# Retention steps over seven side steps instead of four, and mixer outputs in DRAM by halves

## The chip, the cores and the metric

The kernel runs on one core of one Trainium2 chip, in one launch. The metric is device time in microseconds. TensorE is called PE, VectorE DVE, ScalarE ACT, GpSimd POOL, SyncE SP, as in the profile.

## The reference

A hybrid decoder layer on 2048 tokens of width 1024, with 16 learned meta tokens in front, all float32:

```python
h = layer_norm(concat([meta, x]), ln_in)
u, q, k, v, g = split(h @ w_in)            # 256, then 4 x 768 (6 heads of 128)
y_s5  = s5_mixer(u)                        # 16 groups of 16 channels, 64 complex states, scan over tokens
y_ret = retention_mixer(q, k, v, g)        # per head, chunks of 128 tokens, below
h = layer_norm(alpha * h + concat([y_s5, y_ret]) @ w_out, ln1)
h = layer_norm(alpha * h + square(relu(h @ w_up)) @ w_down, ln2)   # d_ff = 4096
return h[:, 16:]

# retention, for a chunk, after rotating q and k:
scores = (q @ k.T) * dmat                  # decayed causal mask
out    = scores @ v + (q @ state) * xi
state  = gamma ** 128 * state + (k * zeta).T @ v
y      = silu(g) * group_norm(out)
```

## The kernel before

**Blocks and phases.** The tokens are worked in two blocks of 1024 (8 tiles of 128 tokens). For each block phase 1 makes the mixers' outputs, phase 2 the output projection with the residual and ln1, phase 3 the MLP. In phase 1 the six heads follow one another: for each tile of a head 24 matmuls make q, k and v (each float32 product is three matmuls of split operands, `mm3`), then `ret_start` begins the retention of that tile; after the fourth and the eighth tile `gates` makes the gate of 512 tokens with 24 more matmuls (in block 1's first head both gates come first).

**The order by hand.** All engines work in program order, which the kernel writes itself. `tick()` is called at set places between matmuls: for a tile once after its first 12 matmuls and once behind `ret_start`; for a gate after 12 matmuls and at its end; in `phase2_open` after the marked products. A tick raises `now`, runs the functions that `defer(k, fn)` has put down for that time or before, the one with the lowest time first, moves the background work (`bg`: the S5 mixer) by one step (`pump`), and feeds weights: a DMA into `wraw`, a cast on ACT and a subtraction on DVE or POOL (L205, L207). In block 0 a gate of the heads after the first has one more pump.

**Retention of a tile.** `ret_start` (L641) scales v on ACT and rotates q and k on DVE (L651 to L654), then defers stage b by 2: two transposes into a bank `pt` of the `sm` pool and a copy on ACT (L666). Stage c, 1 later: scores and k-v product into one bank `pS` (L671, L672), the masked scores `sT` on DVE (L674). Stage d, 1 later: the output into `pO` (L680, L681), the update of the state R from `pS` (L682), statistics and a copy into `o4` (L685 to L687). With the fourth tile of a half `group_norm` follows: a power on POOL, the scaling 2 later, and 4 later the transposes (L718), the affine map on ACT (L720), the product with the gate on DVE (L722) and, one tick on, the store of `y` to DRAM (L723). `meta_head` starts R from the 16 meta tokens, its matmul (L636) 2 ticks behind (1 in the first head).

**Buffers.** PSUM has two pools of four banks, `big` and `sm`. Four retention tiles, norm transposes and S5's matmuls share `sm`; the `big` banks take projections. `o4` has one buffer, `qk` two, `v2` three, `sT` and `qkT` two.

**S5.** `s5_prepare` builds the matrices of the 16 groups in block 0, with one sm bank `pk` a group; `s5_run` then runs them, up to three side by side, each with a bank `pa` (L1035) in its third step and `py` (L1067) in its sixth; a new group starts every 2 steps in block 0, every 4 in block 1. At the end it stores the S5 output (L1134) from `y5o`, one buffer.

**Into phase 2.** `phase2_ahead` loads the mixer outputs of tiles 0 and 1 for the heads that are done; `phase2_split` splits them; `phase2_open` drains S5, runs the products of the first seven channel groups (KORDER) for four groups of sums, flushes all deferred functions, and only then loads and splits the last one (head 5). `phase2` loads ln1's weights, tile 2 (eight DMAs, L1202), the residual tiles (L1207), finishes the open groups (L1211), and splits tile 2 (L1140) behind the first two.

Of the kernel before, what the change touches and what calls it, by code (L numbers as in the profile page):

```python
# [19 lines left out]
NM = 16  # L20
# [30 lines left out]
class Builder:  # L51
# [315 lines left out]
    def build(self):  # L367
        nc, a = self.nc, self.a
        with self.tc.manual_schedule():
# [13 lines left out]
            self.h_d = [dt(f"h{t}", [128, D]) for t in range(NB * NT)]  # L383
            self.y_d = [[dt(f"y{b}_{k}", [128, TB]) for k in range(8)] for b in range(NB)]
            self.s_d = [[dt(f"sum{b}_{x}", [128, 4, 2, 512]) for x in range(5)] for b in range(NB)]
# [230 lines left out]
    def meta_head(self, h, part):  # L616
        nc, p1 = self.nc, self.p1
        ps = self.big()
        mh, ml = self.mT
        self.mm3(ps[:NM, :256], [(mh[:, k, :], ml[:, k, :], part(k, 0, 128, 384), part(k, 1, 128, 384))  # L620
                                 for k in range(8)])
        c, s = self.ropem[:, 0:64], self.ropem[:, 64:128]
        t1 = p1.tile([NM, 2, 64], F32, tag="t1", name="mt1")
        t2 = p1.tile([NM, 2, 64], F32, tag="t2", name="mt2")
        km = p1.tile([NM, 2, 64], F32, tag="qk", name="mk", bufs=2)
        vm = p1.tile([NM, 128], F32, tag="v2", name="mv", bufs=3)
        kin = ps[:NM, 0:128].rearrange("p (a d) -> p a d", a=2)
        nc.scalar.activation(out=vm, in_=ps[:NM, 128:256], func=AF.Copy, scale=self.cols[:NM, 24 + h:25 + h])
        nc.vector.tensor_tensor(out=t1, in0=kin, in1=c.unsqueeze(1).to_broadcast([NM, 2, 64]), op=ALU.mult)
        nc.vector.tensor_tensor(out=t2, in0=kin, in1=s.unsqueeze(1).to_broadcast([NM, 2, 64]), op=ALU.mult)  # L630
        nc.vector.tensor_tensor(out=km[:, 0, :], in0=t1[:, 0, :], in1=t2[:, 1, :], op=ALU.subtract)
        nc.vector.tensor_tensor(out=km[:, 1, :], in0=t1[:, 1, :], in1=t2[:, 0, :], op=ALU.add)

        def fin():
            pr = self.sm()
            nc.tensor.matmul(pr[:, :128], km.rearrange("p a d -> p (a d)"), vm, start=True, stop=True)  # L636
            nc.scalar.copy(self.R[h], pr[:, :128])
        self.defer(1 if h == 0 else 2, fin)


    def ret_start(self, b, h, t, ps):  # L641
        nc, p1 = self.nc, self.p1
        v2 = p1.tile([128, 128], F32, tag="v2", name="v2", bufs=3)
        nc.scalar.activation(out=v2, in_=ps[:, 256:384], func=AF.Copy, scale=self.cols[:, h:h + 1])
# [3 lines left out]
        t2 = p1.tile([128, 4, 64], F32, tag="t2", name="t2")  # L648
        qk = p1.tile([128, 4, 64], F32, tag="qk", name="qk", bufs=2)
        src = ps[:, 0:256].rearrange("p (a d) -> p a d", a=4)  # L650
# [4 lines left out]
        q = qk.rearrange("p a d -> p (a d)")  # L655
        if t % 4 == 0:
            self.o4 = p1.tile([128, 4, 128], F32, tag="o4", name="o4")
            self.mv4 = self.small([128, 4, 2], "gn_mv", 3)
        o4, mv4 = self.o4, self.mv4

        def stage_b():
            pt = self.sm()
            nc.tensor.transpose(pt[:, 0:128], q[:, 0:128], self.ident)
            nc.tensor.transpose(pt[:, 128:256], q[:, 128:256], self.ident)
            qkT = p1.tile([128, 256], F32, tag="qkT", name="qkT", bufs=2)
            nc.scalar.copy(qkT, pt[:, 0:256])  # L666
            self.defer(1, lambda: stage_c(qkT))

        def stage_c(qkT):
            pS = self.sm()  # L670
            nc.tensor.matmul(pS[:, 0:128], qkT[:, 128:256], qkT[:, 0:128], start=True, stop=True)  # L671
            nc.tensor.matmul(pS[:, 128:256], q[:, 128:256], v2, start=True, stop=True)  # L672
            sT = p1.tile([128, 128], F32, tag="sT", name="sT", bufs=2)
            nc.vector.scalar_tensor_tensor(out=sT, in0=pS[:, 0:128], scalar=float(GAMMA[h] ** -128),  # L674
                                           in1=self.mask, op0=ALU.mult, op1=ALU.mult)
            self.defer(1, lambda: stage_d(qkT, pS, sT))

        def stage_d(qkT, pS, sT):
            pO = self.sm()
            nc.tensor.matmul(pO[:, 0:128], sT, v2, start=True, stop=False)  # L680
# [9 lines left out]

        self.defer(2, stage_b)

# [8 lines left out]
    def group_norm(self, b, h, nb, o4, mv4):  # L701
# [6 lines left out]
        def scale():  # L708
            nc.vector.tensor_scalar(out=sc, in0=sc, scalar1=self.cols[:, 6 + h:7 + h], scalar2=None, op0=ALU.mult)
            for i in range(4):  # L710
                nc.vector.tensor_scalar(out=o4[:, i, :], in0=o4[:, i, :], scalar1=mv4[:, i, 0:1],
                                        scalar2=sc[:, i:i + 1], op0=ALU.subtract, op1=ALU.mult)
        self.defer(2, scale)

        def fin():
# [6 lines left out]
            nc.vector.tensor_tensor(out=y, in0=y, in1=self.sgate.pop((b, h, nb)), op=ALU.mult)  # L722
            self.defer(1, lambda: nc.sync.dma_start(out=self.y_d[b][2 + h][:, nb * 512:(nb + 1) * 512], in_=y))  # L723
        self.defer(4, fin)

# [159 lines left out]
    def s5_prepare(self):  # L885
# [33 lines left out]
        def group(g):  # L919
# [9 lines left out]
            def double(k):  # L929
# [18 lines left out]
            yield  # L948
            pk = self.sm()
            flat = lambda z: z.rearrange("p m c -> p (m c)")  # L950
# [4 lines left out]
            yield  # L955
            V.tensor_tensor(out=kz[:, 0:GC], in0=pk[:GC, 0:GC], in1=dd[:, g, :], op=ALU.add)
            S.copy(kz[:, GC:128], pk[:GC, GC:128])
# [13 lines left out]
        nc.sync.dma_start(out=dT, in_=a["s5_dT"])  # L971
        dd = p1.tile([GC, NG, GC], F32, name="dd")
        V.tensor_tensor(out=dd, in0=self.ident[:GC, :GC].unsqueeze(1).to_broadcast([GC, NG, GC]),
                        in1=dT.unsqueeze(2).to_broadcast([GC, NG, GC]), op=ALU.mult)
        self.swap = p1.tile([128, 128], F32, name="swap")
# [46 lines left out]
    def s5_group(self, b, g, y):  # L1022
# [6 lines left out]
        if b == 0:  # L1029
            uT = p1.tile([128, 130], F32, tag="uTm", name="uTm", bufs=3)  # L1030
            S.copy(uT[:, :128], self.uT[:, g])
            S.copy(uT[:, 128:130], self.umT[:, g])
# [39 lines left out]
    def s5_run(self, b):  # L1072
# [46 lines left out]
        for oc in range(2):  # L1119
            on = p1.tile([128, TB], F32, tag="misc", name="y5o")  # L1120
            onv = on.rearrange("p (c j) -> p j c", j=8)
            for n in range(2):
# [10 lines left out]
                yield  # L1133
            nc.sync.dma_start(out=self.y_d[b][oc], in_=on)  # L1134

# [9 lines left out]
    def y_load(self, b, ks):  # L1145
        for k in ks:
            self.nc.sync.dma_start(out=self.yraw[:, :, k, :],
                                   in_=self.y_d[b][k][:, 0:256].rearrange("p (t c) -> p t c", t=2))

# [16 lines left out]
    def phase2_open(self, b):  # L1166
# [5 lines left out]
        k0 = self.cover  # L1172
        self.y_load(b, KORDER[k0:7])
        for t, hf in groups:
            ps = self.open[t, hf] = self.big()
            self.mm3(ps, self.out_pairs(t, hf, 0, k0), marks=(1, 3, 6), last=False)
        if k0 < 7:
            for t in range(2):
                self.y_split(raw[:, t, 0:2], 0, 2, self.ys[t])
            for t, hf in groups:  # L1180
                self.mm3(self.open[t, hf], self.out_pairs(t, hf, k0, 7), marks=(1,), first=False, last=False)
        self.flush()
        self.y_load(b, KORDER[7:])
        for t in range(2):
            self.y_split(raw[:, t, 7:8], 7, 8, self.ys[t])

    def out_pairs(self, t, hf, k0, k1):
# [4 lines left out]
    def phase2(self, b):  # L1192
# [6 lines left out]
        def load(t):  # L1199
            raw = self.stp.tile([128, 8, 128], F32, tag="tmp", name="yraw", bufs=2)  # L1200
            for k in range(8):
                nc.sync.dma_start(out=raw[:, k, :], in_=self.y_d[b][k][:, t * 128:(t + 1) * 128])  # L1202
            return raw
# [360 lines left out]
```

## Time and profile before

| | |
|---|---|
| median of 3 runs | 2450.3 us (2446.16 to 2452.24) |
| profiled execution | 2449.24 us, its span 2447.5 us |
| granted clock, mean of the span | 0.987 |
| phase 1 of block 0, of block 1 | 0 to 510 us, 1280 to 1690 us |
| DVE, POOL busy | 66%, 11% |
| DMA | 313.13 MB, 128 GB/s over the span |

The profile page gives each engine's busy time as a share of the span, and the span in 40 slices; the trace answers who waited for whom, what ran in a stretch, and in what order. In rows of an order of time the number in brackets is how long that engine stood idle before the operation, with the operation that released it. "PEld" is PE's weight load, "SPq" a DMA issue on SP. A granted clock of 1.00 is 2.4 GHz, the other level is 1.2 GHz.

### The profile page before, as it was taken

The page shows a single profiled execution, that of the slowest core. Times are in us where ns is not written, and L with a number is a line of the kernel's source. Part 1 is how long each engine was busy: PE and PEld are TensorE (multiplying, and loading weights), DVE is VectorE, ACT ScalarE, POOL GpSimd, SP SyncE. Part 2 cuts the span into 40 slices and gives each one's busy share as a digit, 9 for nine tenths or more (in the row PEclk, how much of TensorE's full clock was granted, in tenths as well). Part 3 has the DMA queues.
Part 4 walks back from the last instruction along what each step waited for, and adds up shares of the span by engine and source line. Part 5 has one row for each costly group of instructions (what it writes and reads, how often), then busy time and mean ns, then how long its engine had stood idle before and what let it go on. Part 6 is the DMA issues. An engine that isn't in the chain of part 4 may idle for free. (4 is left out here: it accounts for less than half of the span.)

```text
span 2447.5 us, 31696 instructions
## 1 busy us (share of the span) xinstructions
PE 2344.7 (96%) x11596; PEld 2007.5 (82%) x11596; DVE 1615.6 (66%) x3491; ACT 668.4 (27%) x1431; POOL 263.4 (11%) x334
## 2 busy tenths in 40 slices
PE   6889999899999999999999999999999999999998
PEld 5778889778878888888888999987887888888886
DVE  6867757666867776766585455565686666566657
ACT  3323323222321232123232222222232122212222
POOL 2322222301000000000030011100100000000004
PEclk8999999999999999999999999999999999999999
DMA  5132253352464546453442322234246343434332
GB/s 202 66 103 83 87 116 114 91 169 73 138 241 146 167 161 202 141 165 112 146 164 92 89 75 79 78 101 153 74 139 239 114 155 112 137 113 155 112 129 86
DMA packets 166972, 313.13 MB, mean 128 GB/s; under 512 B 18544, under 2 KB 59280, under 8 KB 166560
## 3 DMA queue, kind: packets, MB, share of 16 engines
q1 hardware_dynamic: 166816, 311.11, 39.4%
q8 instruction: 91, 1.49, 0.3%
q14 instruction: 65, 0.53, 0.1%
HBM read 256.25 MB, written 55.84 MB: 128 GB/s over the span
## 5 line engine op out<-in xcount | busy, mean ns | idle before, releaser
L357 PE MATMUL big<-pg,act 128*128 128x384 f32 x2304 | 457.0, 348 | 0.8 <-ACT act L340 0.6
L357 PE MATMUL big<-act,pg 128*128 128x512 f32 x1632 | 425.1, 395 | 2.4 <-DVE act L341 2.4
L357 PE MATMUL big<-pg,q 128*128 128x512 f32 x1728 | 412.2, 390 | 0.0
L357 PEld LDWEIGHTS big<-pg,act 128*128 128x128 f32 x2304 | 403.4, 192 | 4.7 <-DVE act L341 1.5
L357 PEld LDWEIGHTS big<-pg,q 128*128 128x128 f32 x1728 | 323.8, 188 | 67.1
L357 PEld LDWEIGHTS big<-act,pg 128*128 128x128 f32 x1632 | 303.9, 189 | 66.9 <-DVE act L341 2.9
L357 PE MATMUL sm<-pg,q 128*128 128x512 f32 x1344 | 322.8, 389 | 0.0
L357 PEld LDWEIGHTS sm<-pg,q 128*128 128x128 f32 x1344 | 252.3, 188 | 52.4
L281 POOL TENSOR_TENSOR ln_rs<-ln_rs,mhalf 128x1 f32<-128x1 f32 (+1 forms) x49 | 51.3, 1047 | 1481.5 <-DVE ln_rs L280 1481.4
L357 PE MATMUL sm<-act,pg 128*128 128x512 f32 x672 | 188.7, 389 | 0.0
L357 PE MATMUL big<-pg,yt 128*128 128x512 f32 x768 | 183.2, 397 | 1.6 <-DVE yt L1140 1.5
L207 DVE TENSOR_TENSOR pg<-wraw,pg 128x512 fp32r<-128x512 f32 x238 | 151.6, 688 | 39.7 <-ACT pg L205 39.7
L357 PEld LDWEIGHTS big<-pg,yt 128*128 128x128 f32 x768 | 145.1, 191 | 33.6 <-DVE yt L1140 3.3
L205 ACT CAST pg<-wraw 128x512 fp32r<-128x512 f32 x272 | 153.2, 619 | 68.1 <-DMA wraw<-in_w_down_dram 27.2
L219 ACT CAST pg<-q 128x512 fp32r<-128x512 f32 x112 | 69.4, 622 | 355.8 <-DVE q L216 355.8
L1288 ACT CAST q<-q 128x512 fp32r<-128x512 f32 x128 | 79.5, 621 | 272.3 <-DVE q L1286 257.4
L357 PE MATMUL sm<-q,pg 128*128 128x512 f32 x504 | 144.6, 395 | 7.5 <-DMA q<-sum 4.0
L1456 DVE TENSOR_TENSOR acc<-acc,big 128x512 f32<-128x512 f32 x128 | 87.0, 684 | 94.7 <-PE big L357 94.6
L1290 DVE TENSOR_TENSOR q<-q 128x512 fp32r<-128x512 f32 x128 | 88.7, 693 | 91.9 <-ACT q L1288 89.0
L357 PEld LDWEIGHTS sm<-act,pg 128*128 128x128 f32 x672 | 126.1, 188 | 26.1
L357 PE MATMUL big<-q,pg 128*128 128x512 f32 x504 | 143.8, 394 | 0.0
L220 DVE TENSOR_TENSOR pg<-q,pg 128x512 fp32r<-128x512 f32 x112 | 76.3, 692 | 82.2 <-ACT pg L219 77.8
(235 smaller groups left out, 2915.2 us busy)
## 6 DMA issues: line engine op xcount, KB each, us to landing
q<-sum SPq DMA_DIRECT2D x336, 256.0 KB, 5.3
wraw<-in_wup_dram SPq DMA_DIRECT2D x64, 512.0 KB, 4.0
wraw<-in_w_down_dram SPq DMA_DIRECT2D x64, 512.0 KB, 4.2
wraw<-in_wslab_dram SPq DMA_DIRECT2D x48, 512.0 KB, 3.6
sum<-q SPq DMA_DIRECT2D x64, 256.0 KB, 2.3
smat<-mat SPq DMA_DIRECT2D x32, 256.0 KB, 3.8
wraw<-in_w_out_dram SPq DMA_DIRECT2D x16, 512.0 KB, 3.7
acc<-h SPq DMA_DIRECT2D x16, 512.0 KB, 3.8
```

What stands on the lines that cost most here:

```text
L205: nc.scalar.copy(pg[z][:, 0, :], raw[0][:, z * 512:z * 512 + 512])
L207: e.tensor_tensor(out=pg[z][:, 1, :], in0=raw[0][:, z * 512:z * 512 + 512], in1=pg[z].bitcast(F32)[:, 0, :], op=ALU.subtract)
L219: nc.scalar.copy(pg[:, 0, :], x)
L220: self.post.append(lambda: nc.vector.tensor_tensor(out=pg[:, 1, :], in0=x, in1=pg.bitcast(F32)[:, 0, :], op=ALU.subtract))
L281: nc.gpsimd.tensor_tensor(out=rs[:n, 0:1], in0=rs[:n, 0:1], in1=self.mhalf[:n, 0:1], op=ALU.pow)
L357: nc.tensor.matmul(ps, l, r, start=(i == 0), stop=(i == n - 1), skip_group_check=more)
L1288: nc.scalar.copy(hi, x)
L1290: nc.vector.tensor_tensor(out=lo, in0=x, in1=hi.bitcast(F32), op=ALU.subtract)
L1456: nc.vector.tensor_tensor(out=acc, in0=acc, in1=ps, op=ALU.add)
```

## The change

Stages b, c and d of a tile come 3, 5 and 7 ticks behind `ret_start` (before 2, 3 and 4), with four buffers for `qk` and five for `v2`; `o4` is taken in stage d. The meta matmul comes 4 ticks behind (1 in the first head). Group norm's transposes come at 3.9 (before 4), which at a tick sorts them ahead of a stage d; in the first head of block 1 the scaling comes after 1 tick and the transposes at 1.9. `pk` takes a `big` bank. The table `dd` goes: its product is made in the operation that adds it. `uTm` has two buffers. The mixer outputs lie in DRAM as tiles of 512 tokens, the S5 output is stored in two parts, and the last head's channel group of tiles 0 and 1 is loaded with the others, and split before the flush.

```diff
-            self.y_d = [[dt(f"y{b}_{k}", [128, TB]) for k in range(8)] for b in range(NB)]
+            self.y_d = [[[dt(f"y{b}_{k}_{n}", [128, 512]) for n in range(2)] for k in range(8)] for b in range(NB)]
...
-        self.defer(1 if h == 0 else 2, fin)
+        self.defer(1 if h == 0 else 4, fin)
...
-        v2 = p1.tile([128, 128], F32, tag="v2", name="v2", bufs=3)
+        v2 = p1.tile([128, 128], F32, tag="v2", name="v2", bufs=5)
...
-        qk = p1.tile([128, 4, 64], F32, tag="qk", name="qk", bufs=2)
+        qk = p1.tile([128, 4, 64], F32, tag="qk", name="qk", bufs=4)
...
-            self.defer(1, lambda: stage_c(qkT))
+            self.defer(2, lambda: stage_c(qkT))
...
-            self.defer(1, lambda: stage_d(qkT, pS, sT))
+            self.defer(1.9, lambda: stage_d(qkT, pS, sT))
 
         def stage_d(qkT, pS, sT):
+            if t % 4 == 0:
+                self.o4 = p1.tile([128, 4, 128], F32, tag="o4", name="o4")
+                self.mv4 = self.small([128, 4, 2], "gn_mv", 3)
+            o4, mv4 = self.o4, self.mv4
...
-        self.defer(2, stage_b)
+        self.defer(3, stage_b)
...
-        self.defer(2, scale)
+        tight = b > 0 and h == 0
+        self.defer(1 if tight else 2, scale)
...
-            self.defer(1, lambda: nc.sync.dma_start(out=self.y_d[b][2 + h][:, nb * 512:(nb + 1) * 512], in_=y))
-        self.defer(4, fin)
+            self.defer(1, lambda: nc.sync.dma_start(out=self.y_d[b][2 + h][nb], in_=y))
+        self.defer(1.9 if tight else 3.9, fin)
...
-            pk = self.sm()
+            pk = self.big()
...
-            V.tensor_tensor(out=kz[:, 0:GC], in0=pk[:GC, 0:GC], in1=dd[:, g, :], op=ALU.add)
+            V.scalar_tensor_tensor(out=kz[:, 0:GC], in0=self.ident[:GC, :GC], scalar=dT[:, g:g + 1], in1=pk[:GC, 0:GC],
+                                   op0=ALU.mult, op1=ALU.add)
...
-            uT = p1.tile([128, 130], F32, tag="uTm", name="uTm", bufs=3)
+            uT = p1.tile([128, 130], F32, tag="uTm", name="uTm", bufs=2)
...
-            nc.sync.dma_start(out=self.y_d[b][oc], in_=on)
+            for n in range(2):
+                nc.sync.dma_start(out=self.y_d[b][oc][n], in_=on[:, n * 512:n * 512 + 512])
...
-        self.y_load(b, KORDER[k0:7])
+        self.y_load(b, KORDER[k0:])
...
-        self.flush()
-        self.y_load(b, KORDER[7:])
         for t in range(2):
             self.y_split(raw[:, t, 7:8], 7, 8, self.ys[t])
+        self.flush()
```

## Rows read from the trace of the kernel before

**Rows 1.** The page's busy times, share of the span, instructions:
```profile
PE 2344.7 (96%) x11596; PEld 2007.5 (82%) x11596; DVE 1615.6 (66%) x3491; ACT 668.4 (27%) x1431; POOL 263.4 (11%) x334
```

**Rows 2.** Whom PE waited for, whole span: us in total, times, longest:
```profile
PE sm L663 <- DVE qk L654: 22.6, 13, 4.9
PE sm L680 <- DVE sT L674: 13.3, 7, 3.6
...
PE sm L636 <- DVE mk L632: 9.2, 2, 7.5
...
PE sm L671 <- ACT qkT L666: 4.1, 3, 2.6
...
PE sm L680 <- DVE zi L1054: 3.5, 2, 1.7
...
PE sm L663 <- DVE gn_sc L709: 1.6, 1, 1.6
PE big L357 <- DVE yt L1140: 1.5, 3, 0.9
```

**Rows 3.** Two windows: busy us of PE, PEld, DVE, ACT, POOL; clock, DMA share, GB/s:
```profile
140.00:150.00 10.00, 2.87 (x9) 2.68 (x10) 3.10 (x13) 0.33 (x2) 3.24 (x13) 0.60 0.39 115
1670.00:1680.00 10.00, 6.87 (x28) 5.45 (x26) 6.59 (x17) 3.27 (x7) 1.01 (x1) 0.83 0.61 200
```

**Rows 4.** Order of time, 470 to 473 us: start, us, engine, line, operation:
```profile
470.31 2.53 POOL L207 TENSOR_TENSOR pg<-wraw,pg 128x512 fp32r<-128x512 f32 x2 [1.76 <-ACT pg L205]
470.55 1.18 DVE L653 TENSOR_TENSOR qk<-t,t 128x128 f32<-128x128 f32 x1
471.65 1.35 DVE L654 TENSOR_TENSOR qk<-t,t 128x128 f32<-128x128 f32 x1
...
473.05 0.47 PE L663 MATMUL sm<-ident,qk 128*128 128x128 f32 x1 [4.29 <-DVE qk L654]
```

**Rows 5.** Order of time, block 1's first head, 1333 to 1337 us:
```profile
1333.52 0.27 ACT L687 COPY o<-sm 128x128 f32<-128x128 f32 x1 [5.10 <-PE sm L718]
...
1336.88 0.48 PE L663 MATMUL sm<-ident,qk 128*128 128x128 f32 x1 [3.40 <-DVE qk L654]
```

**Rows 6.** Order of time, block 0's second head, 146 to 147 us:
```profile
146.10 0.07 DVE L904 MEMSET t<- 128x16 f32 x1 [5.70 <-issue]
...
147.13 0.76 PE L636 MATMUL sm<-mv,mk 16*128 16x128 f32 x2 [7.47 <-DVE mk L632]
```

**Rows 7.** Order of time, an end tick with S5 work and the next, 362 to 369 us:
```profile
362.86 0.38 PE L671 MATMUL sm<-qkT 128*128 128x128 f32 x2
...
363.30 0.39 PE L1035 MATMUL sm<-uTm,smat 128*128 128x130 f32 x2
...
363.67 2.35 PE L357 MATMUL big<-pg,act 128*128 128x384 f32 x12
...
364.66 0.28 DVE L674 SCALAR_TENSOR_TENSOR sT<-sm,mask 128x128 f32<-128x128 f32 x1
...
368.42 0.46 PE L680 MATMUL sm<-v,sT 128*128 128x128 f32 x2 [1.74 <-DVE zi L1054]
```

**Rows 8.** Order of time, block 1, from phase 1 into phase 2:
```profile
1683.30 15.05 PE L357 MATMUL big<-pg,yt 128*128 128x512 f32 x65
1683.59 0.78 ACT L720 ACTIVATE yst<-sm,gnc 128x512 f32<-128x512 f32 x1 [6.45 <-PE sm L718]
...
1685.12 0.33 SPq L723 DMA_DIRECT2D y<-yst  x1
...
1698.02 1.22 DVE L1140 TENSOR_TENSOR yt<-yraw,yt 128x1024 fp32r<-128x1024 f32 x1
...
1699.30 5.05 PE L357 MATMUL big<-pg,yt 128*128 128x512 f32 x21 [0.94 <-DVE yt L1140]
```

**Rows 9.** Order of time, block 0's end of phase 1, 506 to 509 us:
```profile
506.69 1.08 DVE L1131 TENSOR_TENSOR y5o<-yst,y5T 128x512 f32<-128x512 f32 x1 [5.40 <-DMA y<-y5o]
...
508.63 0.77 PE L680 MATMUL sm<-v,sT 128*128 128x128 f32 x2 [3.61 <-DVE sT L674]
```

More of the change, by code (lines that the diff above doesn't have):

```diff
@@ L624, in meta_head @@
         t2 = p1.tile([NM, 2, 64], F32, tag="t2", name="mt2")
-        km = p1.tile([NM, 2, 64], F32, tag="qk", name="mk", bufs=2)
-        vm = p1.tile([NM, 128], F32, tag="v2", name="mv", bufs=3)
+        km = p1.tile([NM, 2, 64], F32, tag="qk", name="mk", bufs=4)
+        vm = p1.tile([NM, 128], F32, tag="v2", name="mv", bufs=5)
         kin = ps[:NM, 0:128].rearrange("p (a d) -> p a d", a=2)
@@ L655, in ret_start @@
         q = qk.rearrange("p a d -> p (a d)")
[L656 to L659, printed above, removed]
         def stage_b():
@@ L971, in s5_prepare @@
         nc.sync.dma_start(out=dT, in_=a["s5_dT"])
-        dd = p1.tile([GC, NG, GC], F32, name="dd")
-        V.tensor_tensor(out=dd, in0=self.ident[:GC, :GC].unsqueeze(1).to_broadcast([GC, NG, GC]),
-                        in1=dT.unsqueeze(2).to_broadcast([GC, NG, GC]), op=ALU.mult)
         self.swap = p1.tile([128, 128], F32, name="swap")
@@ L1147, in y_load @@
             self.nc.sync.dma_start(out=self.yraw[:, :, k, :],
-                                   in_=self.y_d[b][k][:, 0:256].rearrange("p (t c) -> p t c", t=2))
+                                   in_=self.y_d[b][k][0][:, 0:256].rearrange("p (t c) -> p t c", t=2))
     def phase2_ahead(self, b):
@@ L1201, in load @@
             for k in range(8):
-                nc.sync.dma_start(out=raw[:, k, :], in_=self.y_d[b][k][:, t * 128:(t + 1) * 128])
+                nc.sync.dma_start(out=raw[:, k, :], in_=self.y_d[b][k][t // 4][:, t % 4 * 128:t % 4 * 128 + 128])
             return raw
```

## Prediction

> **What bounds the kernel now.** I read the page's busy shares first, then whom TensorE (PE) waited for, then those waits cut by stage, and last the order of time around one wait of each kind. PE is busy 96% [rows 1]. What the change moves are small retention matmuls, so what it can win is PE's idle time in front of these, and the clock that such a pause costs. The table of PE's waits [rows 2] has it: 22.6 us at L663 for the rotated q and k, 1.6 there for gn_sc, 13.3 at L680 for the masked scores sT, 9.2 at L636 for the meta keys, 4.1 at L671 for qkT, 3.5 at L680 for the reader of another sm bank: 54 of 2447.5 us, all in the two phases 1 (0 to 510 and 1280 to 1690 us).
>
> The clock: behind such pauses the granted clock is below 1.00 in 8 windows of 10 us after the start-up, the first and the last of them in [rows 3]. 0.83 over 10 us is 3.4 us at 1.2 in place of 2.4 GHz, 1.7 us lost where PE had work.
>
> **What the steps become.** A tile has two ticks, one in the middle of its 24 matmuls and one right behind ret_start. If ret_start(t) runs at tick N, then before: transposes (b) at N+2, scores (c) at N+3, output (d) at N+4; middle, end, middle. Now N+3, N+5 and N+7, all end ticks: one burst a tile with d of tile t-2, b of t and c of t-1, d first because of the 1.9. Each hand-over gains a tick or more, which is 12 matmuls, 2.35 us [rows 7].
>
> **Gains.**
> *q and k.* The 13 waits at L663 are 4.9 us in the start-up, 4.29 [rows 4], 3.40 [rows 5] and ten short ones with 10.0 together, none above 1.8; with gn_sc 12 us, all under the new slack. I take 11. The cause stands in [rows 4]: while GpSimd runs L207, DVE's L653 and L654 take 1.18 and 1.35 us (0.29 is their median), 2.0 us late, inside 2.35. The 4.29 gets 0.4 (d comes first) and 2.35 of new cover, but a 1.9 us wait for sT 9 us ahead of it goes too and brings PE there earlier: of 6.2 us together I take 3.8.
> *The one at 1337* [rows 5] is another thing: ScalarE's copy into o4 (one buffer) waits 5.10 us for group norm's transposes, and v, q and k queue behind it. "tight" puts these transposes ahead of that copy: 3.4.
> *Meta.* DVE stands 5.70 us, behind the store of ucm, and PE 7.47 us [rows 6]. With two ticks more PE does tile 1 first (4.7 us, 2.8 left), then waits in the same burst for tile 0's q and k, which DVE makes behind mk (four operations, some 1.4 us): about 4 stay, 3.5 gained. Not below 0, as the store stays; not above 5, tile 1's work.
> *sT.* One of 3.0 us at 245: 2.6. The two at the phases' ends, 3.61 [rows 9] and 3.1, gain less: a tick there is 6 matmuls of output projection, 1.4 us, and what makes DVE late (5.40 us on the store of y5o [rows 9]; a weight cast) stays. Halving that store leaves both halves to land before the buffer is free. 2.0 for both.
> *Start-up* (0 to 100 us, some 12 us of these waits): the next step there is a transpose of x, whose normalisation ends about when the q and k do, so most reappears: 2, of 0 to 5.
> *Clock*: 6 of the windows' 15 us ((1 - clock) x 10, summed); PE was idle in part of them, and some pauses stay.
> *Old bank waits* (3.5 for zi and smaller ones): 3, as the allocations change order.
> Sum 11 + 3.8 + 3.4 + 3.5 + 2.6 + 2 + 2 + 6 + 3 = 37.
>
> **Costs.**
> *PSUM.* sm has four banks, and [rows 7] shows how they pass on: at 368.42 the fifth tile in a row (scores, pa, norm transposes, b, d) waits for the reader of pa, not of the scores, which are still needed. The bank that has been free longest is taken. The scores' bank was held for one tick, now for two. In a burst of d, b and c these take the three free banks, and what S5 asks for next is the bank whose last reader is d's update of R, on DVE, behind the four rope operations. In [rows 7] the operation at that place (L674) ends 2.08 us after the end tick's start (364.66 + 0.28 - 362.86); PE, with 0.44 for c (362.86 to 363.30), as much for d and half for b, is at S5's matmul at 1.10: 1.0 us each. How often: bursts of all three come twice per half head (its fourth tile and the gate behind it). Half a head has 11 side steps in block 0 and 10 in block 1; S5's 32 allocations stand on each of 37 steps there (37/11 x 2 = 7) and on half of 64 here (64/10 x 2 / 2 = 6): 13, and 15 us with DVE's backlog in block 0. Bounds: 0 if the bank is another; all 31 S5 allocations at end ticks at 1.3 us (1.0, and 1.9 for one tile in six as in [rows 4]), 40. I take 15, the count of the steps. Where group norm's transposes head the burst, c gets their bank and waits for L720 (0.78 us [rows 8]), which ends 1.4 us after the burst's start where PE is there at 1.24: 0.2 x 22 = 4. pk goes to big, four banks with two claims a tile: 0, at most 16 x 0.25.
>
> In the Trainium skill, Perfetto Trace Analysis, Optimization Strategy, a gap that repeats over a stretch on the engine that should be full can mean that PSUM or SBUF has no room for the next tile. That speaks against a change that holds a bank longer and adds none. No such regular gap is in this trace (3.5 us in two waits, [rows 2]); if each of the 96 bursts paid 1.0 us for it the sum would be 2523, the third rival carried to its end.
>
> *Start of phase 2.* Nothing covers this one. The last head's output is stored when its group norm ends; SP issues ln1's weights, the eight loads of tile 2 and the h tiles behind that store, and from there to tile 2's split it is one chain, 1685.12 to 1699.24, 14.1 us [rows 8]. PE meanwhile works at open groups of the output projection, from 1683.30 on 66 matmuls at 0.229 us ((15.05 - 0.39)/64) until it needs tile 2. Now group norm ends at tick N+11 in place of N+8, three ticks or 21 matmuls later: PE's lead shrinks by 4.8 us, the chain by the load of y7 that goes (0.43): 0.94 becomes 5.3 us. In block 0 no wait was there and the lead was just used up: 4.4. Together +8.8, and 2 for the clock behind two such pauses: 10.8. Loading y7 early only touches the 1.5 us of [rows 2].
>
> *The rest.* dd is one DVE operation less; the four S5 stores become eight, 0.42 us of SP each, beside 15 us of PE work; uTm with two buffers makes ScalarE's copy wait for PE's last read: 0, at most 16 x 0.3, as ScalarE is busy 27% [rows 1].
>
> Costs 15 + 4 + 10.8 = 30, net -7. Some 10 us of retention waits stand in the gains as staying (4 meta, 2 to 3 at 473, 4 at the ends), and a PE that stalls for R lets DVE catch up, so the two are partly the same time: I take 5 back, -12. The profiled execution took 2449.2 us (span 2447.5, 1.7 around it), 1 below the median 2450.3: 2437.
>
> **Rivals.**
> *Nearly all kept.* R's update comes early enough, or S5 gets another bank, and phase 2's loads catch up: 2449 - 37 = 2412. For: the ten waits are short. Against: [rows 8] is a chain in SP's order.
> *No net change.* Rope is slowed where the burst waits for it: L653 and L654 lose 2.0 us where L207 runs on GpSimd [rows 4], and now R, the statistics and sT all stand behind them. That is so in about one tile in six of block 0; if it meets all seven stalls there, 7 x 1.9 = 13 us more, 2450. In the Trainium skill, SBUF — State Buffer, SBUF: two separate sides, the port pair that DVE and GpSimd share is an exclusive lock, and a DVE operation with two SBUF inputs stands for the whole of a GpSimd operation; [rows 4] agrees (two GpSimd operations in 2.53 us, two DVE operations in 2.53).
> *Slower.* The banks decide: every S5 allocation at an end tick waits for R, 40, with 4 and 10.8 against 37: +18, 2467. It decides from about 20 stalls of 1.3 us on. For: an S5 bank was held up to 5 us (363.30 to 368.42, [rows 7]). Against: a burst without all three steps leaves an older bank.
>
> **How the numbers follow.** Forecast 0.45, all kept 0.20, no change 0.20, slower 0.15. One measurement tells about 0.3% (7 us) from no change. The forecast's own spread, 2425 to 2446, is below 2443 for 0.39 of its 0.45; with the first rival faster has 0.59, same 0.06 + 0.17, slower 0.18. The range 2409 to 2464 cuts off the outer ends of the first and third rival.
>
> **What would show it.** Right: PE's waits for qk at L663 and sT at L680 fall from 36 to under 12 us, L636 to 4 or less in block 0's second head; PE waits at S5's matmuls (L1035, L1067 of before) for R of L682, about 13 times; a wait of 4 to 5 us for yt of L1140 at each start of phase 2. Wrong: no wait for R (first rival) or over 20 (third); waits for yt below 2 us; retention waits that stay.

## The result: slower by 1.3%

The changed kernel took 2482.4 us (median of 4 runs, 2479.3 to 2487.2) against 2451.1 for the kernel before beside it: ratio 1.0133, 95% interval 1.0111 to 1.0156. The forecast was 2437 and its range ended at 2464, so it was wrong in sign and out of range. The profiled execution has a span of 2485.4 us, near the upper end of its runs; it is set against the 2447.5 of before, a difference of 37.9 (the medians differ by 31.3).

The busy times, to be laid beside [rows 1]:

```profile
PE 2363.2 (95%) x11596; PEld 2021.6 (81%) x11596; DVE 1605.2 (65%) x3490; ACT 663.7 (27%) x1431; POOL 267.9 (11%) x334
```

The same 11596 matmuls keep PE busy 18.5 us longer. That is clock: the mean granted clock fell from 0.987 to 0.979, and (1 - clock) x span is 31.8 us before and 52.2 after. The other 19.4 us are new idle time of PE. So in these two executions about half of the loss is waiting and half a slower clock.

Where it is, by stage. Both spans are cut at the same matmuls of L357, numbers 1950, 4950 and 6750 in PE's order (the stretches are block 0's and block 1's phase 1 with the start of phase 2); columns as in [rows 3]. Before:

```profile
0.00:570.20 570.20, 502.94 (x2858) 445.81 (x2859) 395.38 (x1248) 169.09 (x500) 152.36 (x208) 0.97 0.37 114
...
1268.60:1730.80 462.20, 445.57 (x2546) 407.51 (x2545) 261.04 (x725) 121.71 (x280) 52.76 (x67) 0.99 0.32 96
```

After:

```profile
0.00:594.10 594.10, 514.94 (x2859) 454.99 (x2860) 388.43 (x1247) 166.81 (x500) 150.23 (x208) 0.95 0.36 109
...
1292.30:1769.80 477.50, 453.80 (x2546) 413.45 (x2545) 258.47 (x725) 119.42 (x280) 59.80 (x67) 0.97 0.31 93
```

Block 0's stretch is 23.9 us longer, block 1's 15.3, the rest 1.3 shorter. Whom PE waited for in the changed kernel, to be laid beside [rows 2]:

```profile
PE sm L667 <- ACT yst L721: 10.8, 17, 6.3
PE big L952 <- DVE v L945: 9.7, 5, 5.7
...
PE sm L680 <- DVE sT L670: 8.5, 3, 3.7
...
PE sm L1125 <- DVE R L682: 7.1, 2, 5.7
PE sm L1034 <- ACT uTm L1031: 5.8, 2, 5.3
PE sm L1125 <- DMA y5T<-s5y: 5.5, 1, 5.5
PE big L357 <- DVE acc L1210: 5.3, 2, 3.0
PE sm L1034 <- DVE R L682: 4.2, 8, 0.6
...
PE sm L1066 <- DVE R L682: 3.1, 2, 2.1
PE sm L636 <- DVE mk L632: 2.7, 2, 2.3
...
PE sm L659 <- DVE qk L654: 1.0, 1, 1.0
```

(L659 is L663 of before, L667 is L671, L670 is L674, L721 is L720, L952 is L951, L1034 is L1035, L1125 is L1126.) The waits that the change aimed at went in large part: rotated q and k from 22.6 to 1.0 us, the meta keys from 9.2 to 2.7, sT from 13.3 to 8.5. In their place stand four kinds that hardly existed before:

- *R in front of S5's matmuls* (12 times, 14.4 us) and *yst in front of the scores* (17 times, 10.8 us): a PSUM bank that is not free yet.
- *y5T, uTm* (11.3 us): PE stands in front of S5's DMA transfers; the copy that makes uTm waits for the loads of u (first row below).
- *v of L945* (9.7 us, 1.2 before: second row): S5's preparation.
- *acc* (5.3 us): the start of phase 2.

```profile
337.96 0.30 ACT L1030 COPY uTm<-uT 128x128 f32<-128x128 f32 x1 [6.91 <-DMA uT<-u]
...
PE sm L951 <- DVE v L944: 1.2, 4, 0.7
```

The longest wait for R, in order of time (start, us, engine, line, operation):

```profile
513.95 0.91 SPq L1134 DMA_DIRECT2D y<-y5o  x2
...
514.67 0.39 PE L681 MATMUL sm<-R,qkT 128*128 128x128 f32 x2
...
515.33 0.39 PE L668 MATMUL sm<-v,qk 128*128 128x128 f32 x2
519.56 1.08 DVE L1130 TENSOR_TENSOR y5o<-yst,y5T 128x512 f32<-128x512 f32 x1 [5.16 <-DMA y<-y5o]
...
521.08 0.28 DVE L682 SCALAR_TENSOR_TENSOR R<-R,sm 128x128 f32<-128x128 f32 x1
...
521.41 2.93 PE L1125 MATMUL sm<-y5T,wglu 128*128 128x512 f32 x3 [5.69 <-DVE R L682]
```

DVE waits 5.16 us for the store of y5o, as it did before (5.40, [rows 9]). Behind it in DVE's queue stands the update of R (521.08). In the burst d, b, c at 514.5 to 515.7 three sm banks were taken; the fourth is the one with the older tile's scores and R's addend, which R's update still has to read. The gated unit's matmul asks for it and stands 5.69 us. Before, the same wait of DVE reached PE at sT, for 3.61 us ([rows 9]).

Another, in block 1, same columns:

```profile
1618.82 1.10 PE L719 MATMUL sm<-ident,o 128*128 128x128 f32 x4 [1.34 <-DVE o L711]
...
1625.42 0.63 ACT L1095 ACTIVATE gt<-gt 128x512 f32<-128x512 f32 x1 [2.60 <-DVE gt L1094]
...
1626.21 0.77 ACT L721 ACTIVATE yst<-sm,gnc 128x512 f32<-128x512 f32 x1
...
1627.03 0.79 PE L667 MATMUL sm<-qkT 128*128 128x128 f32 x2 [6.31 <-ACT yst L721]
```

Group norm's transposes head the burst at 1618.82. ScalarE's read of that bank (L721) is queued behind two tanh of S5's gelu, which wait for DVE and GpSimd. The scores at the burst's end are handed just that bank and wait 6.31 us. The clock in the windows around these two pauses (columns as in [rows 3]):

```profile
515.00:525.00 10.00, 4.31 (x12) 2.06 (x11) 2.36 (x6) 0.79 (x3) 0.00 (x0) 0.73 0.28 103
1622.00:1632.00 10.00, 4.97 (x14) 4.10 (x15) 7.35 (x17) 3.36 (x7) 1.15 (x1) 0.51 0.07 27
```

0.51 over 10 us is nearly all of them at 1.2 GHz in place of 2.4.

### The profile page after: what moved, and what is told of

Its sections match the earlier page's. It is cut to its first block, busy times and chain, and to the rows that moved or that the text cites. A ratio compares the mean times of both kernels' runs of the same rounds, so it can differ in the third digit from the quotient of the medians.

```text
span 2485.4 us, 31672 instructions
## 1 busy us (share of the span) xinstructions
PE 2363.2 (95%) x11596; PEld 2021.6 (81%) x11596; DVE 1605.2 (65%) x3490; ACT 663.7 (27%) x1431; POOL 267.9 (11%) x334
## 5 line engine op out<-in xcount | busy, mean ns | idle before, releaser
L357 PE MATMUL big<-pg,act 128*128 128x384 f32 x2304 | 447.6, 347 | 0.3 <-ACT act L340 0.3
L357 PE MATMUL big<-act,pg 128*128 128x512 f32 x1632 | 426.5, 398 | 2.6 <-DVE act L341 2.6
L357 PE MATMUL big<-pg,q 128*128 128x512 f32 x1728 | 412.3, 390 | 0.0
L357 PEld LDWEIGHTS big<-pg,act 128*128 128x128 f32 x2304 | 408.2, 194 | 2.4 <-issue 1.0
L357 PEld LDWEIGHTS big<-pg,q 128*128 128x128 f32 x1728 | 323.8, 188 | 67.1
L357 PEld LDWEIGHTS big<-act,pg 128*128 128x128 f32 x1632 | 308.2, 191 | 69.8 <-issue 3.5
L357 PE MATMUL sm<-pg,q 128*128 128x512 f32 x1344 | 322.8, 389 | 0.0
L357 PEld LDWEIGHTS sm<-pg,q 128*128 128x128 f32 x1344 | 252.2, 188 | 52.4
L357 PE MATMUL big<-pg,yt 128*128 128x512 f32 x768 | 189.6, 406 | 6.9 <-DVE acc L1210 5.3
L357 PE MATMUL sm<-act,pg 128*128 128x512 f32 x672 | 188.7, 389 | 0.0
L357 PEld LDWEIGHTS big<-pg,yt 128*128 128x128 f32 x768 | 148.3, 196 | 41.6 <-issue 7.2
L357 PE MATMUL sm<-q,pg 128*128 128x512 f32 x504 | 144.0, 394 | 7.9 <-DMA q<-sum 7.9
L357 PEld LDWEIGHTS sm<-act,pg 128*128 128x128 f32 x672 | 126.1, 188 | 26.0
L651 DVE TENSOR_TENSOR t<-big,rope 128x256 f32<-128x256 f32 x96 | 40.6, 422 | 160.6 <-ACT v L644 160.4
L357 PE MATMUL big<-q,pg 128*128 128x512 f32 x504 | 142.8, 392 | 0.0
```

Source lines behind the costliest of these rows:

```text
L357: nc.tensor.matmul(ps, l, r, start=(i == 0), stop=(i == n - 1), skip_group_check=more)
L651: nc.vector.tensor_tensor(out=t1, in0=src, in1=c, op=ALU.mult)
```

## The experiments

Theory A: PE, freed of its retention waits, runs ahead into S5's own chain (its DMA round trips, the store of y5o) and into the late group norm. Theory B: the sm banks that are held over two steps decide. A first question was which part of the change does it. The times (five rounds each, beside the kernel before, 2447.7 to 2449.0 us):

| Run | us | ratio to before | 95% |
|---|---|---|---|
| halves_alone | 2449.3 | 1.0005 | 0.9996–1.0013 |
| steps_alone | 2486.5 | 1.0157 | 1.0141–1.0172 |
| tight_alone | 2444.8 | 0.9983 | 0.9974–0.9992 |
| s5_big | 2461.3 | 1.0048 | 1.0034–1.0062 |
| before_s5_big | 2443.8 | 0.9978 | 0.9967–0.9990 |
| norm_big | 2475.5 | 1.0112 | 1.0099–1.0126 |
| s5_norm_big | 2449.1 | 0.9998 | 0.9989–1.0007 |
| d_soon | 2446.1 | 0.9994 | 0.9985–1.0003 |
| norm_soon | 2444.9 | 0.9985 | 0.9976–0.9993 |
| two_y5o | 2446.4 | 0.9992 | 0.9982–1.0001 |
| s5_early | 2447.0 | 0.9998 | 0.9989–1.0007 |
| s5_early2 | 2438.3 | 0.9962 | 0.9950–0.9975 |
| new_best | 2439.1 | 0.9961 | 0.9949–0.9974 |
| old_best | 2441.0 | 0.9970 | 0.9959–0.9981 |
| new_best2 | 2430.3 | 0.9926 | 0.9914–0.9938 |
| d_best | 2435.4 | 0.9952 | 0.9939–0.9966 |
| old_best2 | 2441.7 | 0.9977 | 0.9968–0.9986 |

**Which part of the change.** halves_alone is before with the change of the DRAM tiles:

```
-  self.y_d = [[dt(f"y{b}_{k}", [128, TB]) ...
+  self.y_d = [[[dt(f"y{b}_{k}_{n}", [128, 512]) for n in range(2)] ...
-  self.y_load(b, KORDER[k0:7])    # and the last block after flush()
+  self.y_load(b, KORDER[k0:])     # flush() moved behind the splits
```

> The kernel before with only the DRAM halves, the eight S5 stores and the early load of the gate's last channel block; the retention steps as before. Theory A (the loss is made by the retention steps that come later): 2446 to 2454 us, the kernel before within 0.2%, PE's wait at the start of phase 2 of block 1 stays at 0.9 us or falls by up to 0.4. Rival (the doubled stores hold y5o and the queue of SP longer): 2456 to 2465, with DVE's wait for the store of y5o in front of L1131 up from 5.4 to over 6 us and the wait for sT behind it up from 3.6.

steps_alone is after with that taken back:

> The kernel after with its mixer outputs kept whole in DRAM again, four S5 stores and the late load; the retention steps spread over seven. Theory A (steps): 2478 to 2488 us, within 0.2% of the kernel after, with the waits for y5T (5.5 us), R in front of the gated unit (5.7) and acc (3.0 and 2.4) all still there. Rival (halves and the early load carry a part): 2455 to 2470.

The halves change nothing, and the steps are as slow without them (1.0157, if anything more). Both theories had this in common: the loss is made by the seven steps. (steps_alone also holds the small edits of S5: pk, dd, uTm. They were not run apart. PE's wait for uTm, at least, is one for a transfer and not for its buffers, as shown above.)

tight_alone is before with the one piece for block 1's first head:

```
+        tight = b > 0 and h == 0
-        self.defer(2, scale)
+        self.defer(1 if tight else 2, scale)
-        self.defer(4, fin)
+        self.defer(1.9 if tight else 4, fin)     # o4 taken in stage_d
```

> The kernel before with only the earlier group norm of block 1's first head and o4 taken at the output step. By the prediction's own step 3.4 us go at 1337: 2445 to 2449, with ScalarE's wait of 5.1 us in front of L687 there gone and PE's wait of 3.4 at the transposes behind it under 0.5. Rival (the wait only moves to another reader of that bank or to the next half head): 2450 to 2454, with a new wait of 2 to 4 us between 1335 and 1350.

0.17% is 4.2 us (1.9 to 6.3): the 3.4 of the prediction stand.

**Which banks.** s5_big gives S5's tiles (all in after) another set of banks:

```
-        pa = self.sm()        # and py, and the gated unit's pg
+        pa = self.big()
```

> The kernel after with all of S5's PSUM tiles (pa, py and the gated unit) on the four big banks, so that they no longer take the banks that the scores held until R's update. Theory B (sm banks held for R decide): the 12 waits for R, 14.4 us together, go with their low clock, 2460 to 2466 us. Theory A (PE runs ahead of S5's own chain: the round trip of y5T through DRAM, the store of y5o, and the late group norm): the short waits for R go (some 5 us), the 5.7 us in front of the gated unit turns into a wait for sT or for the reader of the unit's own bank, the waits for y5T and at the start of phase 2 stay: 2472 to 2480.

It won 1.0133 - 1.0048 = 0.85%, 21 us, which is theory B's number, though the waits for R hold only 14.4. Between the profiled executions it is 22.1 us, of which 18.4 are idle time of PE and 3.7 busy time, and the mean clock is 0.980 in place of 0.979: what came back here was mostly waiting. The trace of s5_big has no wait for R left; what else stands there:

```profile
PE sm L667 <- ACT yst L721: 11.3, 18, 6.3
PE sm L680 <- DVE sT L670: 10.9, 4, 3.7
...
PE big L1034 <- DMA smat<-mat: 5.7, 1, 5.7
```

The control is the same edit in the kernel before:

> The control to the run s5_big: the kernel before, retention in four steps, with S5's three PSUM tiles on the big banks. If the bank that is held for R is what S5 paid for in the kernel after, there is little to win here: only the 5 us of waits for zi and yst at S5's and d's banks, 2442 to 2447 us. Rival (S5 is better off on big whatever the steps, for instance because the big banks come free sooner): a gain near the 21 us that the kernel after had, 2427 to 2433.

0.22%, 5 us: where the scores' bank is held for one step there is little to win. norm_big and s5_norm_big move group norm's transposes, the first in after, the second in s5_big:

```
-            pn = self.sm()
+            pn = self.sm() if h == NH - 1 and nb else self.big()
```

> The kernel after with only group norm's transposes moved to a big bank (except a block's last ones); S5 stays on sm. If the two bank costs are separate (s5_big won 21 us, the norm bank another 12 on top of it), the 17 waits for yst at the scores (10.8 us) go and 12 us are won alone: 2466 to 2473. Rival (taking one tile from the sm banks makes S5 get an older bank too): the waits for R fall as well, from 14.4 to under 6 us, 2452 to 2462.

> s5_big (2461 us) with group norm's transposes on a big bank as well, except for the last ones of a block. Theory B (the bank decides): the 18 waits of the scores for ScalarE's read of the norm bank, 11.3 us with the 6.3 us one, go with the clock behind the long one: 2448 to 2453. Theory A (ScalarE is late there anyway, behind the tanh of S5's gelu, and its next reader is the transposed q and k): the sixteen short ones go (some 4 us), the 6.3 us one comes back as a wait for qkT of 2 to 4 us: 2455 to 2459.

On top of s5_big the norm bank is worth 0.50%, 12 us, and the kernel is level with before; theory A's guess, that the 6.3 us would come back as a wait for qkT, was wrong. PE's busy time is 17.5 us lower than in s5_big (2342.0 and 2359.5) and the mean clock 0.985, but these two executions stand at opposite ends of their runs. Alone the norm bank won 0.21%, 5 us, inside the intervals. With the norm tile off the sm banks the waits for yst go, but S5 still waits for R, mostly at the same matmuls and as much in all:

```profile
PE sm L1125 <- DVE R L682: 7.8, 2, 5.9
...
PE sm L1034 <- DVE R L682: 5.1, 7, 1.0
...
PE sm L1066 <- DVE R L682: 3.3, 2, 2.2
```

16.2 us against 14.4. The measured 2475.5 lies above both expectations for norm_big. It looks as if the two costs were not separate, but 5 against 12 us is no more than the intervals leave open.

**The hold itself.** d_soon leaves all tiles where they are and moves one number of after:

```
-            self.defer(1.9, lambda: stage_d(qkT, pS, sT))
+            self.defer(1, lambda: stage_d(qkT, pS, sT))
```

> The kernel after with the output step one side-work step behind the scores (3, 2 and 1 steps; the bank of the scores held for one step, as in the kernel before), every tile on the sm banks. Theory B (the bank held for two steps is what S5 pays for): the 12 waits of S5's matmuls for R, 14.4 us in the kernel after, go or fall under 3 us, 2456 to 2466 us, near s5_big's 2461; the waits for yst stay. Rival (R is late because DVE is late, whatever the steps): waits for R of 8 us or more stay, 2472 to 2484.

1.0133 - 0.9994 = 1.39%, 34 us: the whole loss, more than either theory allowed. Its trace:

```profile
PE sm L680 <- DVE sT L670: 24.1, 15, 3.8
...
PE sm L667 <- ACT yst L721: 0.7, 1, 0.7
```

No wait for R is left and 0.7 of 10.8 us for yst at the scores, though neither S5's tiles nor the norm tile have another set of banks. But the one number does two things. The scores' bank comes back one step earlier, and d, with group norm ahead of it, leaves the burst for the middle tick. In order of time:

```profile
336.03 0.60 PE L719 MATMUL sm<-ident,o 128*128 128x128 f32 x4
...
343.74 0.39 PE L667 MATMUL sm<-qkT 128*128 128x128 f32 x2
```

The scores come 7.7 us behind group norm's transposes here, and 1.5 us behind them in after (342.77 to 344.24). So d_soon does not show how much is the shorter hold and how much the burst that is split. That the banks alone suffice, s5_norm_big shows: it reaches the same time with d and group norm where after has them. What d_soon pays is sT, 24.1 us in place of 8.5.

**Where the gains went.** s5_norm_big and d_soon have next to no bank waits, and are level with before. (Against before_s5_big, whose S5 tiles are on the same banks, s5_norm_big is even 0.20% slower, at the edge of the intervals.) The trace of s5_norm_big:

```profile
PE sm L680 <- DVE sT L670: 14.5, 7, 4.3
...
PE big L952 <- DVE v L945: 8.6, 7, 4.2
PE big L1125 <- DMA y5T<-s5y: 6.4, 1, 6.4
...
PE big L357 <- DVE acc L1210: 5.7, 2, 3.3
PE big L1034 <- DMA smat<-mat: 5.3, 1, 5.3
```

So theory A's waits are the second half of the story. norm_soon and two_y5o take two of them on, over s5_norm_big:

```
-        tight = b > 0 and h == 0
+        tight = (b > 0 and h == 0) or (h == NH - 1 and nb == 1)
```

> s5_norm_big with the last head's second group norm scaled one step and transposed two steps behind the output step in place of two and four. If the late group norm sets the start of phase 2, the two waits for acc there (2.5 us each in s5_big, with 1.4 for yt and their low clock) go or fall under 1 us, against one wait of 1 to 2 us for the scaled o at each transposes: 4 to 9 us less than s5_norm_big. Rival (the chain through SP's queue sets it, whenever group norm ends): within 2 us of s5_norm_big, the acc waits above 2 us.

```
+            if oc:     # two tiles of 512 in the tag of stab, one in misc
+                ons = [p1.tile([128, 512], F32, tag="stab", ...) for _ in range(2)]
```

> s5_norm_big with the second half of the gated unit's output in buffers of its own (its product in two operations of half the size), so that DVE has no wait for the store of the first half. DVE's wait in front of L1130 (5.2 us in the kernel after) goes in both blocks; with it PE's wait for sT near 515 (2.4 us in s5_big) and the one near 1690 (3.7 in the kernel after): 4 to 8 us less than s5_norm_big. Rival (PE then only waits for the next late thing, the start of phase 2): within 2 us of s5_norm_big, the waits for acc longer by what was won.

norm_soon won 0.13% (3 us), the acc waits fell from 5.7 to 1.3 us (those for yt rose from 1.6 to 2.4); two_y5o won 0.06%, inside the intervals, and the acc waits stayed (5.3); why it won no more is not shown. s5_early moves S5's chain in block 0:

```
-            yield                      # gelu: a step each quarter
+            if b or q % 2:
+                yield
     um = self.ffp.tile([2, NG, 8, GC], F32, tag="ff", name="um")
+    self.u_load(0)                     # was: after the transposes of um
```

> s5_norm_big (2449 us) with S5's own chain ahead by three steps: in block 0 the gelu takes two quarters a step, and the loads of u are issued before the reads of the meta rows are waited for. If the pauses that are left in block 0 (6.4 us for y5T at the gated unit, 5.3 us for smat at S5's first group) are PE standing in front of S5's DMA chains, they fall under 1.5 us each, with their low clock: 2437 to 2442. Rival (DVE is full there and the gelu in fewer steps makes sT and the rope late): the two waits shrink by less than 3 us together or waits for sT and qk of block 0 grow as much, 2446 to 2452.

The waits for y5T and smat went, but the time did not move, by a mistake of the experiment: the eight loads of u stood ahead of the small load of um in SP's queue.

```profile
PE sm L995 <- DMA um<-um: 9.0, 1, 9.0
```

s5_early2 has them behind it:

> s5_early with the loads of u behind the small load of the meta rows in SP's queue. If PE's pauses in front of S5's DMA chains are what took the gains back: no wait for um over 1 us, the wait for smat at S5's first group (5.3 us) under 2, the one for y5T stays away: 2436 to 2441. Rival (PE only waits for the next link): a wait of 3 us or more for uTm, stab or sT in the same places, 2444 to 2449.

0.9962: 0.36%, 9 us from two pauses of 6.4 and 5.3 us; a wait of 1.5 us for um is what is left of them. It bears theory A out for block 0. new_best and new_best2 add norm_soon and two_y5o to these; d_best is new_best2 with d_soon's number; old_best is before with tight_alone and s5_big, old_best2 before with everything that new_best2 has except the seven steps, their buffers, the later meta matmul and the small edits of S5 (pk, dd, uTm):

> s5_early with the last head's earlier group norm and the second buffer of the gated unit's output as well: what spreading over seven steps can bring where banks and S5's chain are out of its way. Theory B: the three gains are in different places and add up, 2430 to 2438, faster than before by 0.4 to 0.8%. Rival (each is taken back at the next stage): 2441 to 2447, no better than norm_soon alone.

> The kernel before with the same help that needs no spreading: S5's tiles on big and block 1's earlier first group norm. The two single runs gave -0.22 and -0.17%: 2438 to 2442 if they add. If this is as fast as new_best, the seven steps themselves bring nothing even without the bank waits; if it is over 4 us slower, the spreading is worth that.

> s5_early2 with the last head's earlier group norm and the second buffer of the gated unit's output; seven steps. By the gain that these two had over s5_early (8 us): 2428 to 2434. Rival (no better than new_best): 2436 to 2441.

> new_best2 with the output one step behind the scores (six steps). If the seventh step only costs, 2 to 6 us less than new_best2; if it gains where the banks are out of its way, the waits for sT (14 us in new_best, 24 in d_soon) come back and it is 5 to 10 us slower than new_best2.

> The kernel before, four steps, with all the help of new_best2: S5 and group norm on big banks, the gelu in fewer steps, the loads of u earlier, halves in DRAM with the second buffer of the gated unit, the earlier group norm of block 1's first head and of the last head. If the gains that the prediction counted for the spreading (the waits for qk, the meta keys and sT) are real once nothing takes them back, this stays 8 to 16 us behind new_best2's 2430: 2438 to 2446. Rival (the help does it all, and the steps bring nothing): 2428 to 2434.

new_best2 beats both kernels: 2430.3 us, 0.74% under before. Here norm_soon and two_y5o together are worth 0.36% (0.9962 to 0.9926), against 0.19% for the two one by one, a difference inside the intervals. The same help without the spreading gives 0.9977, so the seven steps, with the edits named, are worth 0.51%, 12 us, once less is in their way: old_best2 still waits 17.3 us for qk and 8.9 for the meta keys, new_best2 1.0 and 3.0. d_best's six are 0.26% slower than seven, its sT waits are back:

```profile
PE sm L680 <- DVE sT L670: 28.5, 17, 7.6
```

## Why the prediction was wrong

Its sum was 37 of gains against 30 of costs (15 and 4 for banks, 10.8 for phase 2), with 5 of these taken off as counted twice. Step by step:

- *q and k, 11 + 3.8.* The waits went as foretold, to 1.0 us. That 11 of them would be won was wrong: see the last point.
- *tight, 3.4.* Right (4.2 measured).
- *Start-up, 2 of 12.* It came back at the next transposes of x, as foretold, and more: the waits for x (L295) went from 4.7 to 9.3 us, and matmul 300 of L357 starts at 115.8 us, before at 112.9.
- *Meta, 3.5.* The wait fell by 6.5 us and the one for v of L945 rose by 8.5. In order of time, block 0's second head in after:

```profile
147.43 0.07 DVE L905 MEMSET t<- 128x16 f32 x1 [4.74 <-DMA u<-ucm]
...
148.45 0.45 PE L636 MATMUL sm<-mv,mk 16*128 16x128 f32 x2 [0.38 <-DVE mk L632]
...
154.91 0.45 POOL L915 TENSOR_TENSOR t<-t,tb 128x128 f32<-128x128 f32 x1
...
158.11 0.59 PE L952 MATMUL big<-v,s5b 128*16 128x128 f32 x2 [5.70 <-DVE v L945]
```

  The meta keys now cost 0.38 us where [rows 6] had 7.47. But the same store also holds the powers t that GpSimd forms next (to 155.4); behind them in GpSimd's order stand the operations that start v, which S5's first matmul needs: 5.70 us. The prediction stopped one link short.
- *sT, 4.6.* 4.8 less, but the number is luck. The wait near 245, of which 2.6 were to go, is still 2.10 (at 252); the one at block 1's end is 3.73 in place of 3.13. The 3.61 of [rows 9] went, to the gated unit.
- *R's banks, 15.* 12 waits with 14.4 us against "13, and 15" came out near in part by luck. At the pa and py that it counted there are ten with 7.3 us, three in block 0 (7 foretold) and seven in block 1 (6 foretold), eight of them 0.5 us and not 1.0. The other two, 7.1 us, are at the gated unit, which it did not count: 5.69 came where R's update stood behind the store of y5o, a wait that [rows 9] shows and that the prediction used only for sT. Moving these banks gave 21 us back.
- *Group norm to scores, 4.* Mis-sized most: 10.8 us. Fifteen of the 17 waits are the foretold 0.20 us; two, of 6.31 and 1.46, make the difference. In the longer one a tanh that waited for DVE stood ahead of the read in ScalarE's order. The 6.45 us that ScalarE waited ahead of L720 in [rows 8] said nothing of its queue elsewhere.
- The two bank terms, 19 us, are 33 by s5_norm_big (27 to 39 with the intervals), and 34 by d_soon, which splits the burst as well.
- *Clock, 6 won.* Wrong in sign: 31.8 us at (1 - clock) x span became 52.2. Waits of over 5 us went from two to six.
- *Start of phase 2, 10.8.* Right in mechanism, too large in size: waits for acc and yt of 4.0 us in block 0 and 2.8 in block 1, where 4.4 and 5.3 were foretold. They show at acc, the residual rows (L1206) queued behind the loads of tile 2, more than at yt; norm_soon won 3 us there. In order of time, block 0:

```profile
548.59 1.33 SPq L1206 DMA_DIRECT2D acc<-h  x3
...
552.71 1.28 DVE L1210 SCALAR_TENSOR_TENSOR acc<-acc,big 128x512 f32<-128x512 f32 x2 [9.45 <-DMA acc<-h]
553.54 1.03 PE L357 MATMUL big<-pg,yt 128*128 128x512 f32 x2 [2.96 <-DVE acc L1210]
...
555.18 1.22 PE L357 MATMUL big<-pg,yt 128*128 128x512 f32 x2 [0.61 <-DVE yt L1140]
```

- *What had no term: S5's DMA chain.* "What is late next" was asked of the retention's own operations and not of S5's. In block 0 the removed waits had been cover for it. SP's queue at the gated unit, after:

```profile
485.67 6.50 SPq L1108 DMA_DIRECT2D s5y<-y  x8
...
495.39 0.88 SPq L1114 DMA_DIRECT2D y5T<-s5y  x2
...
501.51 3.75 PE L1125 MATMUL sm<-y5T,wglu 128*128 128x512 f32 x4 [5.54 <-DMA y5T<-s5y]
```

  From the first store to the matmul it is 15.8 us. The same way in the kernel before:

```profile
473.62 6.31 SPq L1109 DMA_DIRECT2D s5y<-y  x8
...
489.97 1.88 PE L1126 MATMUL sm<-y5T,wglu 128*128 128x512 f32 x4
```

  It took 16.4 us and PE had no wait at its end: it had lost 4.29 us at qk in [rows 4] and 1.31 more at 486.7. With these gone it came 5.5 us early.

So two steps failed. The bank terms were 19 us, 14 after what was taken off, in place of 33. And the gains, net of phase 2, were to be 26; with the banks out of the way they were 0.5 (s5_norm_big) to 1.5 us (d_soon), no more than the intervals. They were not imaginary: new_best2 against old_best2 has 12 of them. They were won only with the next links, S5's transfers and the last group norm, early too. The rival "Slower" had the mechanism, the banks, but the wrong form: not every S5 allocation, a dozen, a few of them long, and the reads of the norm bank beside them. The signs that the prediction named as proof came true all the same (qk and sT at 9.5 us, 12 waits for R), but for the waits of 4 to 5 us for yt: they watched the waits that were known.

In the Trainium skill, Perfetto Trace Analysis, Optimization Strategy, a gap that repeats on the engine that should be full can mean that PSUM has no room for the next tile. The changed kernel's trace agrees: 17 waits of the scores for a norm bank and 12 of S5 for R. The prediction had set this aside, since the trace of before has no such gap.

Left open: which waits bring the clock down, and how the two bank costs share what they have in common. Between the profiled executions of after and d_soon, 40.4 us apart, 25.3 are idle time of PE and 15.1 busy time.

## To carry to other kernels

Holding a PSUM bank for one step longer is not priced by an average wait: two of the 29 bank waits here hold 12.0 of 25.2 us. Look for the slowest operation that can stand in the queue of the engine that frees the bank. Before a wait is counted as won, follow the next hand-over of everything that ran beside it, DMA round trips included, for the same number of microseconds. Change the hand-over that gains slack (here transposes and qkT) apart from the one that holds a resource (here the scores).

## What was not expected of the hardware

The clock's part. With the new waits came 18.5 us on the busy time of unchanged matmuls, as much as all new idle time, at a mean clock of 0.979 in place of 0.987. Windows of 10 us below 1.00, cut from the span's start, are 29 in place of 16, and their (1 - clock) x 10 is 50 us in place of 29; the windows around the five pauses of 5.3 to 6.3 us hold some 18 of the 50. In two windows around such a pause the clock was 0.73 and 0.51, while in the window from 1356 to 1366, where the pause of [rows 5] is gone, it was 1.00. Long waits alone do not settle it: without the waits for R, s5_big still has 0.979 to 0.983 in its runs.
